# Requested weight groups, mixer products on VectorE, a new start, and Strassen's seven products in the down projection of a hybrid layer

## The chip, the cores and the metric

One Trainium2 chip, one NeuronCore. The metric is the device time of one execution in microseconds, as a median of repeated runs; the profile is of one further execution of the same program. TensorE (PE) multiplies 128x128 stationary tiles with moving tiles of up to 512 columns into PSUM; VectorE (DVE), ScalarE (ACT) and GpSimd (POOL) do elementwise work; SyncE (SP) issues the weight transfers.

## The reference

One layer over x of 256 x 2048 in float32. All sizes below are fixed: 11 chunks of 512 columns make the hidden width 5632.

```python
x = x + 0.5 * swiglu(rmsnorm(x, ffn1_norm), ffn1_w_gate, ffn1_w_up, ffn1_w_down)
h = rmsnorm(x, mix_norm)
x = x + mixer(h, rmsnorm(mem, mem_norm), ...)   # w_in, linear attention, spatial gating,
                                                # attention into 256 memory rows, w_branch, w_out
x = x + 0.5 * swiglu(rmsnorm(x, ffn2_norm), ffn2_w_gate, ffn2_w_up, ffn2_w_down)
return rmsnorm(x, final_norm)

def swiglu(h, w_gate, w_up, w_down):            # (2048, 5632), (2048, 5632), (5632, 2048)
    return (jax.nn.silu(h @ w_gate) * (h @ w_up)) @ w_down
```

## The kernel before

**Products in three parts.** A float32 operand is split into a high part of the type float32r (ACT's cast, `wh`, L119) and a low part (DVE's subtraction, `wl`, L120). A product of two tiles is then three PE matmuls: high x high, high x low, low x high (`products`, L123 to L125; in the Strassen blocks `three`, L364 for all). The weights come from memory in groups of four 128-row tiles by 512 columns (`load`, 1 MB, `raw`, a ring of three), requested on SP, and are split in halves of two tiles (`wh` and `wl`, rings of three). The tokens are two blocks of 128, so each half of a group is used in 12 matmuls.

**A feed-forward block (FFN)** walks over the 11 hidden chunks in parts of 4, 4 and 3 (`ffn`, L454). For each chunk it makes the gate and up products over 16 k tiles, the gated activation, four transposes for each token block (L166) and a split of the result into `hT` (`tsplit`, L174 and L175). After a part's last chunk it multiplies `hT` with the part's rows of `w_down`, for four groups of 512 output columns, and adds half of that into the tokens `x_s` (L486). Chunk 0 uses the plain `gemm`. Chunks 1 to 10 use `gated_strassen` (L348): the first four k tiles of the gate and of the up weights are taken as a 2 x 2 block matrix against the tokens' 2 x 2 blocks, with seven products (`p1` to `p7`, `seventh`) of sums of blocks instead of eight; the sums of the weight blocks are made on DVE (L413, 1024 columns wide) and split like weights; the sums of the token blocks are made once per FFN (`strassen_forms`, L313). The other 12 k tiles run as plain products (`rest`). The two first weight groups of a chunk (`rg`, `ru`) lie in slots of the pool `big` (17 slots of 8 KB per partition, `m` in the trace) and are requested when the chunk's code begins (L353).

**The mixer** (w_in, three branches, w_branch, w_out) runs small work of its branches in generators, one step at each half group (`tick`). The linear attention has seven levels; each makes two differences on DVE (L810, L811), an exponential on ACT (L812), one product on DVE (L814) and one on POOL (L815), all feeding small PE products (L795) and a masked copy on DVE (L799).

**The start** loads `mem` in four pieces and the first groups of `w_kv`; `norm_piece` (L182) transposes a piece on PE and makes its scaled high and low parts tile by tile (L190 on ACT, L191 on DVE). ACT also squares `mem` for the row sums (`mem_stats`, L257).

**Order.** Each engine runs its instructions in a fixed order; the order is made at build time by a scheduler that moves instructions of the program text ahead where their inputs allow. A pool's tile waits for the last reader of the slot it takes; SP and POOL requests wait in their queue for that too.

Of the kernel before, what the change touches and what calls it, by code (L numbers as in the profile page):

```python
# [8 lines left out]
F32 = mybir.dt.float32  # L9
# [50 lines left out]
def layer(ctx: ExitStack, tc: tile.TileContext, a: dict, out: bass.AP):  # L60
# [56 lines left out]

    def split(raw, wh, wl):
        nc.scalar.copy(wh, raw)  # L119
        nc.vector.tensor_tensor(wl, raw, wh.bitcast(F32), op=ALU.subtract)  # L120
# [119 lines left out]
    transposed_gains(gm, slice(0, KT))  # L240
    first = []
    for n in range(NCH):
# [4 lines left out]
        for b in range(NB):  # L247
            norm_piece(part[:, b, :], MEM, memT, None, b, n)
# [63 lines left out]

    def strassen_forms(xT):  # L313
# [18 lines left out]
    def gated(xT, rs, wg, wu, col):  # L332
# [15 lines left out]
    def gated_strassen(xT, forms, rs, wg, wu, col, between):  # L348


        rg, ru, tt = (slot([P, 4, CW]) for _ in range(3))
        for r, w in ((rg, wg), (ru, wu)):
            nc.sync.dma_start(  # L353
                r, w[: 4 * P, col : col + CW].rearrange("(j p) n -> p j n", p=P)
            )
# [39 lines left out]
        def rest():  # L395

            for g0 in range(4, KT, 4):
                for w, accs in ((wg, (p2, p4)), (wu, (p3, p8))):
                    raw = load(w, g0 * P, col)
                    for h0 in (0, 2):  # L400
                        wh, wl = ring(raw[:, h0 : h0 + 2, :])
                        last = g0 + h0 == KT - 2
# [10 lines left out]
        add = lambda o, x, y: nc.vector.tensor_tensor(o, x, y, op=ALU.add)  # L413
        sub = lambda o, x, y: nc.vector.tensor_tensor(o, x, y, op=ALU.subtract)
# [10 lines left out]

        c11, c21 = tmp(), tmp()
        e = slot([P, 2, CW])
        nc.scalar.copy(c11, p1)
        sub(e[:, 0], p6, c11)
        sub(c21, e[:, 0], p7)  # L430
        add(e[:, 0], e[:, 0], p5)
        add(e[:, 1], c21, p5)
        between()
# [5 lines left out]
        seventh(p4, tile_of(2, 1), own(t3), False)  # L439
        for _ in others:  # L440
            pass
        add(c11, p2, c11)
# [10 lines left out]

    def ffn(xT, rs, wg, wu, wd, after, begin=lambda: None, final=False):  # L454
        done, forms = 0, None
        for part, n_ch in enumerate((4, 4, 3)):
# [8 lines left out]

            for c in range(n_ch):
                col = (done + c) * CW
                if done + c == 0:
                    tiles = gated(xT, rs, wg, wu, col)
                    forms = strassen_forms(xT)  # L470
                else:
                    tiles = gated_strassen(xT, forms, rs, wg, wu, col, turn)
# [3 lines left out]
            if part == 2:  # L476
                begin()
            for n in range(NCH):
# [5 lines left out]
                for b in range(NB):  # L484
                    xs = x_s[b][:, n * CW : (n + 1) * CW]
                    nc.vector.scalar_tensor_tensor(  # L486
                        out=xs, in0=pd[b], scalar=0.5, in1=xs, op0=ALU.mult, op1=ALU.add
                    )
# [133 lines left out]
    def spatial():  # L622
# [14 lines left out]
        for b in range(NB):  # L637
# [9 lines left out]
            nc.gpsimd.tensor_tensor(sv[:, b, :], sv[:, b, :], ln[:, 1, :], op=ALU.add)  # L647
# [135 lines left out]
    def linear_attention():  # L783
# [22 lines left out]
        for i, m in enumerate(LEVELS):  # L806
# [8 lines left out]
            nc.gpsimd.tensor_tensor(qk[:, 1], kT, e, op=ALU.mult)  # L815
# [59 lines left out]
    for b in range(NB):  # L875
        nc.gpsimd.tensor_tensor(r_s[:, b, :], r_s[:, b, :], on, op=ALU.mult)
# [103 lines left out]
```

## Time and profile before

| | |
|---|---|
| median of 3 runs | 2377.97 us (2376.36 to 2378.29) |
| profiled execution | 2376.76 us; its span from first to last instruction 2375.1 us |
| PE busy | 2348.6 us, 99% of the span |
| PE weight loads (beside the products) | 1940.5 us, 82% |
| DVE busy | 1527.3 us, 64% |
| ACT busy | 1136.7 us, 48% |
| POOL busy | 63.1 us, 3% |
| moved by DMA | 456 MB, mean 192 GB/s |

Busy shares are averages over the whole span. A PE instruction's own length (0.39 us for 512 columns) overlaps with its neighbours', so the pace is read from the distance between starts. `[x <-ENGINE ...]` behind a row is the idle time of the engine before it and what ended it.

### The profile page before, as it was taken

Reading aid. Unit: us, or ns where it says so; the run is one execution under the profiler, and the core shown is the slowest. Engines: PE = TensorE matmul, PEld = TensorE weight load, DVE = VectorE, ACT = ScalarE, POOL = GpSimd, SP = SyncE. Lnnn points to the kernel's source line nnn. Section 1 sums busy time; section 2 is a strip of 40 time slices with the busy share of each in tenths; the row PEclk is TensorE's granted clock in tenths of the full one; section 3 lists DMA queues with packets and bytes.
Section 4 is the critical chain, followed back from the end, with each engine's and each line's share of the span. In section 5 each row is a group of like instructions: output and inputs, shape, how many; then the busy total and the mean of one; then the engine's idle time right before and its main releaser. Section 6 shows DMA issues by size and latency. Waiting matters only on the chain.

```text
span 2375.1 us, 26552 instructions
## 1 busy us (share of the span) xinstructions
PE 2348.6 (99%) x10610; PEld 1940.5 (82%) x10610; DVE 1527.3 (64%) x1658; ACT 1136.7 (48%) x1347; POOL 63.1 (3%) x62
## 2 busy tenths in 40 slices
PE   8999999999999999999999999999999999999998
PEld 6878888888888888888788888888788888888886
DVE  5668746885676656556765555556677468756765
ACT  6544534554454544435444444445445345534444
POOL 0000000000000001001200000000000000000000
PEclk9999999999999999999999999999999999999999
DMA  7665556655655665444446555555555556556554
GB/s 260 215 224 179 195 185 204 213 181 182 208 191 164 201 216 206 171 158 169 166 160 217 192 194 194 187 186 187 203 181 207 179 195 213 195 177 213 195 178 142
DMA packets 224821, 456.00 MB, mean 192 GB/s; under 512 B 7348, under 2 KB 7416, under 8 KB 223544
## 3 DMA queue, kind: packets, MB, share of 16 engines
q1 hardware_dynamic: 222344, 442.56, 55.4%
q0 software_dynamic: 2352, 11.73, 1.4%
q8 instruction: 83, 1.36, 0.2%
q14 instruction: 42, 0.34, 0.0%
HBM read 447.97 MB, written 6.29 MB: 191 GB/s over the span
## 4 chain that ended last, share of the span: by engine, by line
PE 97%; DMA 1%; ACT 1%; issue 1%; DVE 1%; SPq 0%; ACTq 0%; POOLq 0%; POOL 0%; DVEq 0%
PE acc L364 31%; PE acc L124 19%; PE acc L125 19%; PE acc L123 19%; PE trp L364 2%; PE sml L364 2%; PE trp L166 2%; DMA m<-in_ffn_w_gate_dram 1%; PE sml L795 1%; DVE wl L120 0%; ACT wh L119 0%; PE sml L700 0%; PE sml L728 0%; DMA m<-in_mem_dram 0%; ACT tmp L180 0%
## 5 line engine op out<-in xcount | busy, mean ns | idle before, releaser
L120 DVE TENSOR_TENSOR wl<-raw,wh 128x1024 fp32r<-128x1024 f32 x748 | 928.7, 1243 | 734.5 <-ACT wh L119 732.6
L119 ACT CAST wh<-raw 128x1024 fp32r<-128x1024 f32 x748 | 786.7, 1053 | 1002.5 <-PE acc L125 677.3
L124 PE MATMUL acc<-wl,m 128*128 128x512 f32 x2032 | 796.4, 392 | 1.6 <-DVE wl L120 1.6
L125 PE MATMUL acc<-wh,m 128*128 128x512 f32 x2032 | 792.5, 391 | 0.1
L123 PE MATMUL acc<-wh,m 128*128 128x512 f32 x2032 | 729.4, 392 | 1.8 <-ACT wh L119 0.9
L364 PE MATMUL acc<-wh,m 128*128 128x512 f32 x2080 | 656.8, 391 | 5.8 <-ACT wh L119 5.8
L364 PEld LDWEIGHTS acc<-wh,m 128*128 128x128 f32 x2080 | 392.2, 189 | 87.3 <-ACT wh L119 6.2
L123 PEld LDWEIGHTS acc<-wh,m 128*128 128x128 f32 x2032 | 381.6, 188 | 82.2 <-ACT m L190 2.2
L124 PEld LDWEIGHTS acc<-wl,m 128*128 128x128 f32 x2032 | 382.1, 188 | 81.3 <-DVE wl L120 3.1
L125 PEld LDWEIGHTS acc<-wh,m 128*128 128x128 f32 x2032 | 381.9, 188 | 77.4 <-DVE m L191 0.5
L364 PE MATMUL acc<-wl,m 128*128 128x512 f32 x1040 | 408.0, 392 | 1.2 <-DVE wl L120 1.2
L364 PEld LDWEIGHTS acc<-wl,m 128*128 128x128 f32 x1040 | 196.4, 189 | 42.6 <-DVE wl L120 2.3
L119 ACT CAST m<-m 128x1024 fp32r<-128x1024 f32 x80 | 82.5, 1051 | 31.8 <-DVE m L413 29.7
L120 DVE TENSOR_TENSOR m<-m,m 128x1024 fp32r<-128x1024 f32 x80 | 96.3, 1220 | 0.1
L119 ACT CAST wh<-m 128x1024 fp32r<-128x1024 f32 x60 | 63.2, 1054 | 58.3 <-PE acc L364 51.2
L120 DVE TENSOR_TENSOR wl<-m,wh 128x1024 fp32r<-128x1024 f32 x60 | 73.3, 1222 | 14.8 <-ACT wh L119 14.7
L413 DVE TENSOR_TENSOR m<-m,m 128x1024 f32<-128x1024 f32 x60 | 73.1, 1219 | 0.1
L364 PE MATMUL trp<-m,m 128*128 128x512 f32 x240 | 66.3, 390 | 0.0
L190 ACT ACTIVATE m<-trp,gT 128x128 fp32r<-128x128 f32 x128 | 43.1, 363 | 22.6 <-PE trp L166 13.2
L364 PEld LDWEIGHTS trp<-m,m 128*128 128x128 f32 x240 | 45.2, 188 | 9.4
L174 ACT CAST m<-trp 128x512 fp32r<-128x512 f32 x64 | 36.3, 583 | 28.5 <-PE trp L166 28.5
L191 DVE SCALAR_TENSOR_TENSOR m<-trp,gT,m 128x128 fp32r<-128x128 f32 x128 | 41.4, 346 | 13.2 <-ACT m L190 12.2
(175 smaller groups left out, 1025.3 us busy)
## 6 DMA issues: line engine op xcount, KB each, us to landing
raw<-in_w_in_dram SPq DMA_DIRECT2D x96, 1024.0 KB, 5.0
raw<-in_ffn_w_down_dram SPq DMA_DIRECT2D x88, 1024.0 KB, 5.1
raw<-in_ffn_w_gate_dram SPq DMA_DIRECT2D x68, 1024.0 KB, 5.1
raw<-in_ffn_w_up_dram SPq DMA_DIRECT2D x68, 1024.0 KB, 5.1
raw<-in_w_branch_dram SPq DMA_DIRECT2D x24, 1024.0 KB, 5.1
m<-in_ffn_w_gate_dram SPq DMA_DIRECT2D x20, 1024.0 KB, 7.5
m<-in_ffn_w_up_dram SPq DMA_DIRECT2D x20, 1024.0 KB, 8.5
raw<-in_w_out_dram SPq DMA_DIRECT2D x16, 1024.0 KB, 5.1
```

The source lines that it names most:

```text
L119: nc.scalar.copy(wh, raw)
L120: nc.vector.tensor_tensor(wl, raw, wh.bitcast(F32), op=ALU.subtract)
L123: nc.tensor.matmul(acc, lhsT=lhs.h(kt, b), rhs=wh, start=first, stop=False)
L124: nc.tensor.matmul(acc, lhsT=lhs.h(kt, b), rhs=wl, start=False, stop=False)
L125: nc.tensor.matmul(acc, lhsT=lhs.l(kt, b), rhs=wh, start=False, stop=last)
L166: nc.tensor.transpose(out=ps[:, j * P : (j + 1) * P], in_=src[:, j * P : (j + 1) * P], identity=ident)
L174: nc.scalar.copy(hi, ps)
L190: nc.scalar.activation(dst.h(kt, b), pj, AF.Copy, scale=g)
L191: nc.vector.scalar_tensor_tensor(out=dst.l(kt, b), in0=pj, scalar=g, in1=dst.h(kt, b).bitcast(F32), op0=ALU.mult, op1=ALU.subtract,)
L364: nc.tensor.matmul(o, lhsT=lhs, rhs=rhs, start=o not in opened, stop=stop)
L413: add = lambda o, x, y: nc.vector.tensor_tensor(o, x, y, op=ALU.add)
L795: nc.tensor.matmul(pss[:, h * P : (h + 1) * P], lhsT=ks[:, h, b * P : (b + 1) * P], rhs=qs[:, h, b * P : (b + 1) * P], start=True, stop=True,)
```

## The change

It has five pieces.

- **Requests.** The two first weight groups of a Strassen chunk are requested by a function of their own (`first_four`) during the chunk before: for chunk 1 between the gate and the up products of chunk 0, where the token forms are now made too; for the others behind the seventh of the seven products.
- **Down products.** The block code becomes `block_product`, used by the gated chunks and by `down_strassen`. The latter takes two 512-column groups of `w_down` as the two columns of blocks, for parts 0 and 1 of each FFN (two pairs per part); part 2 stays as it was. The forms of `hT` are made once per part. Sums go straight into `x_s` with a factor of 0.5 or -0.5 (`into_x`).
- **Mixer.** Eleven 128x1024 elementwise operations move from POOL to DVE: two in the spatial gating, seven in the linear attention's levels, two on the gate `r_s`.
- **Start.** Twenty transposes of the identity into an unused PSUM tile stand before the first pieces; `mem_stats` is ordered behind the last cast of the first `w_kv` column group.
- **Norm pieces.** Except for the first piece of `mem`, a piece is scaled in one DVE product over four tiles, cast once on ACT and subtracted once on DVE.

```diff
+    def first_four(w1, w2, row, col1, col2):
+        raws = [slot([P, 4, CW]) for _ in range(2)]
+        for r, w, col in zip(raws, (w1, w2), (col1, col2)):
+            nc.sync.dma_start(
+                r, w[row : row + 4 * P, col : col + CW].rearrange("(j p) n -> p j n", p=P)
+            )
+        return raws
...
-    def norm_piece(src, which, dst, ss, b, n):
+    def norm_piece(src, which, dst, ss, b, n, bulk=True):
...
+        if bulk:
+            t = tmp().rearrange("p (j t) -> p j t", t=P)
+            g = gT[:, which * KT + 4 * n : which * KT + 4 * n + 4]
+            nc.vector.tensor_tensor(
+                t, ps.rearrange("p (j t) -> p j t", t=P),
+                g.unsqueeze(2).to_broadcast([P, 4, P]), op=ALU.mult,
+            )
+            hi, lo = dst.four(4 * n, b)
+            nc.scalar.copy(hi, t)
+            nc.vector.tensor_tensor(lo, t, hi.bitcast(F32), op=ALU.subtract)
+            return
...
+    idle = trp()
+    for _ in range(20):
+        nc.tensor.transpose(out=idle[:, :P], in_=ident, identity=ident)
...
         if c == 0:
-            mem_stats()
+            with tc.issue_after(casts[0].ins):
+                mem_stats()
...
-    def gated(xT, rs, wg, wu, col):
+    def gated(xT, rs, wg, wu, col, between):
...
             nc.scalar.activation(sil[b], pg[b], AF.Silu, scale=rs[:, b : b + 1])
+        between()
         pu = [acc() for _ in range(NB)]
...
-    def gated_strassen(xT, forms, rs, wg, wu, col, between):
-        rg, ru, tt = (slot([P, 4, CW]) for _ in range(3))
-        for r, w in ((rg, wg), (ru, wu)):
-            nc.sync.dma_start(
-                r, w[: 4 * P, col : col + CW].rearrange("(j p) n -> p j n", p=P)
-            )
+    def block_product(xT, n_tiles, forms, raws, w1, w2, row0, col1, col2, middle, prefetch):
+        rg, ru = raws
+        tt = slot([P, 4, CW])
...
+        middle(p1, p6, p7, p5)
         add(t3, t3, b21)
         seventh(p2, tile_of(2, 0), ring(b21), False)
         next(others)
         seventh(p3, form(3), ring(b22), False)
         next(others)
         seventh(p4, tile_of(2, 1), own(t3), False)
+        prefetch()
         for _ in others:
             pass
+        return (p2, p4), (p3, p8)
...
+    def down_strassen(hT, n_tiles, forms, raws, wd, row0, n, prefetch):
+        def middle(p1, p6, p7, p5):
+            v, u = tmp(), tmp()
+            nc.scalar.copy(v, p1)
+            into_x(0, n, v)
+            sub(v, p6, v)
+            sub(u, v, p7)
+            add(v, v, p5)
+            into_x(0, n + 1, v)
+            into_x(1, n, u, -0.5)
+            add(u, u, p5)
+            into_x(1, n + 1, u)
+        banks = block_product(
+            hT, n_tiles, forms, raws, wd, wd, row0, n * CW, (n + 1) * CW, middle, prefetch
+        )
+        for i in range(2):
+            for b in range(NB):
+                into_x(b, n + i, banks[i][b])
...
+            if part < 2:
+                hf = strassen_forms(hT)
+                more = first_four(wd, wd, done * CW, 0, CW)
...
+                down_strassen(hT, 4 * n_ch, hf, more, wd, done * CW, 0, fetch_down)
+                down_strassen(
+                    hT, 4 * n_ch, hf, more, wd, done * CW, 2,
+                    (lambda n: lambda: fetch(n))(done + n_ch),
+                )
+                done += n_ch
+                continue
...
-            nc.gpsimd.tensor_tensor(qk[:, 1], kT, e, op=ALU.mult)
+            nc.vector.tensor_tensor(qk[:, 1], kT, e, op=ALU.mult)
```

How the order of the instructions changes, at three places. First PE, at the end of chunk 0 of the first FFN: L123 to L125 (after: L125 to L127) are the last up products of chunk 0, `trp<-ident,tmp` the transposes of its gated result, L364 (after: L397) products of chunk 1. Before:

```order
L123 MATMUL acc<-wh,m_221 128x512
L124 MATMUL acc<-wl,m_221 128x512
L125 MATMUL acc<-wh,m_223 128x512
L166 MATMUL trp<-ident,tmp 128x128 x8
L364 MATMUL acc<-wh,m_220 128x512 x2
```

After:

```order
L127 MATMUL acc<-wh,m_220 128x512
L397 MATMUL acc<-wh,m_217 128x512 x2
L397 MATMUL acc<-wl,m_217 128x512
L397 MATMUL acc<-wh,m_219 128x512
...
L397 MATMUL acc<-wh,m_219 128x512
L168 MATMUL trp<-ident,tmp 128x128 x4
L397 MATMUL acc<-wh,m_217 128x512 x2
L168 MATMUL trp<-ident,tmp 128x128 x4
```

Twelve products of chunk 1 have moved ahead of the transposes. ACT at the same place (L338, after L365: the gate's Silu of chunk 0; `wh<-m` are casts of a first weight group of chunk 1; `m<-trp`, L174, after L176, are the casts of the transposed result). Before:

```order
L338 ACTIVATE tmp<-acc,rs_219 128x512 x2
L119 CAST wh<-raw 128x1024 x6
L174 CAST m_987<-trp 128x4x128 x2
L119 CAST wh<-m_1337 128x1024
L119 CAST wh<-raw 128x1024 x2
```

After:

```order
L365 ACTIVATE tmp<-acc,rs_216 128x512 x2
L121 CAST wh<-raw 128x1024 x6
L121 CAST wh<-m_1146 128x1024
L121 CAST wh<-raw 128x1024 x2
L121 CAST wh<-m_1146 128x1024
L176 CAST m_952<-trp 128x4x128 x2
```

Four casts for chunk 1 have moved ahead of those of the transposed result. Third, ACT at the program's start (L119, after L121: casts of `w_kv` weights; L190, after L203: high parts of the transposed `mem`; L180: squares of `mem`). Before:

```order
L180 ACTIVATE tmp,ss_m<-m_89 128x512 x2
L190 ACTIVATE m_91<-trp,gT 128x128
L119 CAST wh<-raw 128x1024
L190 ACTIVATE m_91<-trp,gT 128x128 x2
L119 CAST wh<-raw 128x1024
L190 ACTIVATE m_91<-trp,gT 128x128
```

After:

```order
L121 CAST wh<-raw 128x1024 x2
L203 ACTIVATE m_91<-trp,gT 128x128 x4
L121 CAST wh<-raw 128x1024
L203 ACTIVATE m_91<-trp,gT 128x128 x2
```

The squares are gone from here (they follow the eighth cast), and two weight casts stand ahead of the first high part.

## Rows read from the trace of the kernel before

**Rows 1.** The page, busy time of each engine over the span.

```profile
PE 2348.6 (99%) x10610; PEld 1940.5 (82%) x10610; DVE 1527.3 (64%) x1658; ACT 1136.7 (48%) x1347; POOL 63.1 (3%) x62
```

**Rows 2.** Chain of waits: start, length in us, what, number of instructions.

```profile
738.80 25.64 PE acc L364 x113
```

**Rows 3.** Waits of PE over the span: us in total, times, longest.

```profile
PE acc L364 <- ACT wh L119: 5.8, 2, 3.0
...
PE acc L124 <- DVE wl L120: 1.6, 3, 0.9
PE acc L364 <- DVE wl L120: 1.2, 2, 0.7
...
PE acc L123 <- ACT m L190: 0.8, 1, 0.8
```

**Rows 4.** Timeline of PE, end of chunk 0 in the first FFN: start, length.

```profile
153.00 0.60 PE L166 MATMUL trp<-ident,tmp 128*128 128x128 f32 x4
...
157.44 0.73 PE L364 MATMUL acc<-wh,m 128*128 128x512 f32 x2 [2.77 <-ACT wh L119]
...
163.31 0.39 PE L364 MATMUL trp<-m,m 128*128 128x512 f32 x1
```

**Rows 5.** Windows: length, busy us (instructions) by engine, PE's granted clock, DMA.

```profile
153.20:163.30 10.10, 6.20 (x22) 4.38 (x21) 8.97 (x9) 5.34 (x7) 0.00 (x0) 0.83 0.41 152
1686.90:1698.80 11.90, 7.91 (x24) 5.54 (x23) 10.40 (x11) 6.37 (x8) 0.00 (x0) 0.71 0.47 161
```

**Rows 6.** Timeline of PE, end of chunk 0 in the second FFN.

```profile
1686.69 0.60 PE L166 MATMUL trp<-ident,tmp 128*128 128x128 f32 x4
...
1691.41 0.93 PE L364 MATMUL acc<-wh,m 128*128 128x512 f32 x2 [2.99 <-ACT wh L119]
...
1698.83 0.63 PE L364 MATMUL acc<-wh,m 128*128 128x512 f32 x2
```

**Rows 7.** Timeline of ACT, end of chunk 0 in the first FFN.

```profile
153.64 0.59 ACT L174 CAST m<-trp 128x512 fp32r<-128x512 f32 x1 [7.55 <-PE trp L166]
...
155.39 1.04 ACT L119 CAST wh<-m 128x1024 fp32r<-128x1024 f32 x1
```

**Rows 8.** Windows as rows 5: part 0's down products; a gated Strassen chunk.

```profile
540.00:630.00 90.00, 90.00 (x403) 74.61 (x401) 47.64 (x46) 36.77 (x37) 0.00 (x0) 1.00 0.55 182
640.00:682.00 42.00, 42.00 (x187) 34.80 (x186) 32.06 (x32) 21.23 (x22) 0.00 (x0) 1.00 0.55 187
```

**Rows 9.** Groups by line and shape: count, busy us, mean ns, idle before.

```profile
L120 DVE TENSOR_TENSOR wl<-m,wh 128x1024 fp32r<-128x1024 f32 x60 | 73.3, 1222 | 14.8 <-ACT wh L119 14.7
L413 DVE TENSOR_TENSOR m<-m,m 128x1024 f32<-128x1024 f32 x60 | 73.1, 1219 | 0.1
L486 DVE SCALAR_TENSOR_TENSOR m<-acc,m 128x512 f32<-128x512 f32 x48 | 31.0, 683 | 7.8 <-PE acc L125 7.8
L323 DVE TENSOR_TENSOR m<-m 128x256 f32<-128x256 f32 x2 | 0.8, 414 | 0.0
```

**Rows 10.** Timeline of all engines, a level of the linear attention.

```profile
1131.88 3.44 POOL L815 TENSOR_TENSOR m<-m,m 128x1024 f32<-128x1024 f32 x1 [3.52 <-ACT m L812]
...
1132.98 3.43 DVE L120 TENSOR_TENSOR wl<-raw,wh 128x1024 fp32r<-128x1024 f32 x1
...
1136.47 0.50 PE L124 MATMUL acc<-wl,m 128*128 128x512 f32 x1 [0.38 <-DVE wl L120]
```

**Rows 11.** Timeline of PE and ACT at the program's start.

```profile
6.08 1.97 PE L166 MATMUL trp<-ident,m 128*128 128x128 f32 x8 [3.25 <-DMA m<-in_mem_dram]
...
8.68 1.22 PE L123 MATMUL acc<-wh,m 128*128 128x512 f32 x2 [0.62 <-ACT wh L119]
...
9.12 1.04 ACT L119 CAST wh<-raw 128x1024 fp32r<-128x1024 f32 x1
...
10.96 0.63 PE L123 MATMUL acc<-wh,m 128*128 128x512 f32 x1
11.38 1.05 PE L124 MATMUL acc<-wl,m 128*128 128x512 f32 x2
```

More of the change, by code (lines that the diff above doesn't have):

```diff
@@ L116, in load @@
         return raw
+    casts = []
     def split(raw, wh, wl):
-        nc.scalar.copy(wh, raw)
+        casts[:] = [nc.scalar.copy(wh, raw)]
         nc.vector.tensor_tensor(wl, raw, wh.bitcast(F32), op=ALU.subtract)
@@ L247, in layer @@
         for b in range(NB):
-            norm_piece(part[:, b, :], MEM, memT, None, b, n)
+            norm_piece(part[:, b, :], MEM, memT, None, b, n, bulk=n > 0)
         if n < 3:
@@ L395, in rest @@
         def rest():
-            for g0 in range(4, KT, 4):
-                for w, accs in ((wg, (p2, p4)), (wu, (p3, p8))):
-                    raw = load(w, g0 * P, col)
+            for g0 in range(4, n_tiles, 4):
+                for w, col, accs in ((w1, col1, (p2, p4)), (w2, col2, (p3, p8))):
+                    raw = load(w, row0 + g0 * P, col)
                     for h0 in (0, 2):
                         wh, wl = ring(raw[:, h0 : h0 + 2, :])
-                        last = g0 + h0 == KT - 2
+                        last = g0 + h0 == n_tiles - 2
                         for b in range(NB):
@@ L424, in gated_strassen @@
         next(others)
[L426 to L433, printed above, removed]
+        middle(p1, p6, p7, p5)
         add(t3, t3, b21)
@@ L439, in gated_strassen @@
         seventh(p4, tile_of(2, 1), own(t3), False)
+        prefetch()
         for _ in others:
             pass
+        return (p2, p4), (p3, p8)
+    def gated_strassen(xT, forms, raws, rs, wg, wu, col, between, prefetch):
+        c11, c21 = tmp(), tmp()
+        e = None
+        def middle(p1, p6, p7, p5):
+            nonlocal e
+            e = slot([P, 2, CW])
+            nc.scalar.copy(c11, p1)
+            sub(e[:, 0], p6, c11)
+            sub(c21, e[:, 0], p7)
+            add(e[:, 0], e[:, 0], p5)
+            add(e[:, 1], c21, p5)
+            between()
+        (p2, p4), (p3, p8) = block_product(
+            xT, KT, forms, raws, wg, wu, 0, col, col, middle, prefetch
+        )
         add(c11, p2, c11)
@@ L464, in turn, with fetch, make_ready @@
                 waiting.clear()
+            def fetch(c):
+                nonlocal raws
+                if c < 11:
+                    raws = first_four(wg, wu, 0, c * CW, c * CW)
+            def make_ready():
+                nonlocal forms
+                forms = strassen_forms(xT)
+                fetch(1)
             for c in range(n_ch):
@@ L468, in ffn @@
                 if done + c == 0:
-                    tiles = gated(xT, rs, wg, wu, col)
-                    forms = strassen_forms(xT)
-                else:
-                    tiles = gated_strassen(xT, forms, rs, wg, wu, col, turn)
+                    tiles = gated(xT, rs, wg, wu, col, make_ready)
+                else:
+                    more = (lambda n: lambda: fetch(n))(done + c + 1)
+                    tiles = gated_strassen(
+                        xT, forms, raws, rs, wg, wu, col, turn,
+                        more if c < n_ch - 1 else lambda: None,
+                    )
                 waiting.append((c, tiles))
@@ L484, in ffn @@
                 for b in range(NB):
[L485 to L488, printed above, removed]
+                    xs = into_x(b, n, pd[b])
                     if part == 2:
@@ L875, in layer @@
     for b in range(NB):
-        nc.gpsimd.tensor_tensor(r_s[:, b, :], r_s[:, b, :], on, op=ALU.mult)
+        nc.vector.tensor_tensor(r_s[:, b, :], r_s[:, b, :], on, op=ALU.mult)
     gla_gen = linear_attention()
```

21 lines of the change are left out of this document (17 added, 4 removed).

## The prediction

> **What bounds the kernel now.** I read the page first: TensorE (PE) is busy 2348.6 of 2375.1 us, VectorE (DVE) 64%, ScalarE (ACT) 48% [rows 1]. So the kernel is a stream of PE products, and time can come only from fewer products or from the places where the stream breaks. The chain of waits gives the price of one product: 113 of them, one behind the other, take 25.64 us, which is 0.227 us each at the full clock [rows 2]; one product's own 0.39 us is overlapped by its neighbours. The PE's waits say where the stream breaks [rows 3]: 7.0 us in four waits for an ACT cast or a DVE low part at Strassen products (L364), all four at the start of a chunk 1, 1.6 us for DVE's low parts elsewhere, 0.8 us at the start. The waits alone undercount the first of these, since the clock falls behind them, so I looked at the timeline there.
>
> At the end of chunk 0 of the first feed-forward block (FFN) the PE starts eight transposes at 153.00, is then idle 2.77 us up to 157.44, and reaches the first `trp` product at 163.31 [rows 4]. The windows view counts 22 PE instructions in that stretch, at a granted clock of 0.83, and 24 in the like stretch of the second FFN, at 0.71 [rows 5]; the level in between is 1.2 instead of 2.4 GHz for part of the stretch. In the first stretch eight transposes at about 0.1 us and 14 products at 0.227 would need 4.0 us, and 10.3 went by: 6.3 lost. In the second [rows 6], eight and 16 would need 4.4, and 12.1 went by: 7.7 lost. Together 14.0 us. The cause stands on ACT: it is idle 7.55 us until the transposes' result comes, because the casts of that result stand in its queue ahead of the next chunk's weight casts, and the cast of the first weight group begins only at 155.39 [rows 7]. Those transposes in turn wait for the gated product, which is the last thing chunk 0 makes; nothing of chunk 1 stands between.
>
> **The change, part by part.**
>
> *Down products.* A pair of output columns of a four-chunk part now takes 2 x 16 x 2 x 3 = 192 products. By the seven products it takes 7 x 2 x 3 = 42 for the first four k tiles and 12 x 2 x 2 x 3 = 144 for the rest: 186. Two pairs, two parts and two FFNs make eight blocks, so 48 products go, at 0.227 us: **-10.9 us**. This term is sure as long as PE stays the bound. What it costs elsewhere: a block has 19 splits where the pair had 16, four 1024-wide additions at 1.22 us, and twelve 512-wide operations at 0.68 where there were four [rows 9]; DVE so gets about 3 x 1.22 + 4 x 1.22 + 8 x 0.68 = 14 us per block, and 2.4 + 4 x 0.41 = 4.1 us of forms once per part. I price that at nothing, because the PE's 42.2 us per block cover it: the gated Strassen block has the same 19 splits, four additions and nearly as many narrow operations, and there DVE is busy 32.1 of 42 us, while the down stretch now uses 47.6 of 90 [rows 8]. In the gated stretches PE has no wait on the list but the four named [rows 3]. With the forms a part's last gated chunk goes to some 36 of 42. If that cover is gone (an addition ahead of a low part that PE needs), each such place costs a wait like the longest for DVE here, 0.9 us [rows 3], and a wait of 2.8 us costs 6.3 with the clock. Eight block starts are new; I put **+1 us** for all, with 0 and 10 as the ends.
>
> *Requests ahead.* The first weight groups of the next chunk are asked for during the chunk before, and in the new order the PE has twelve rest products of chunk 1 ahead of the transposes, ACT has four weight casts ahead of its two transposed casts. Both links of the chain above are broken. On SP the pair now stands ahead of all eight raw groups of the first FFN's chunk 0, in the second behind two of them (before: behind the third raw group of chunk 1); the raw groups behind it wait for it on SP, but three of them fit in their ring ahead of the PE, some 16 us of products. What is late next is DVE's gated product, which the twelve products (2.7 us) cover. Of the 14.0 us I take **-13.0**, since a low part can still be a little late; the ends are -14 (all of it) and -9 (one of the two keeps two thirds of its loss).
>
> *Mixer operations.* Eleven 128x1024 operations go from GpSimd (POOL) to DVE. Beside POOL's 3.44 us a DVE subtraction that takes 1.22 elsewhere takes 3.43, and a PE wait of 0.38 stands behind it [rows 10]. So DVE already pays about 2.2 us beside such an operation, and would pay 1.2 for doing it: a level of the linear attention is up to 1 us shorter on DVE, which has no idle time before these rows. Against it: two multiplications now stand in one piece ahead of the next low part. The DVE waits there are 1.6 us on the list; I take **-1.5**, with +4 (a wait of 0.9 at each of the five levels that stand close together) and -3 (the listed waits and as much again in ACT's casts behind them) as ends.
>
> *Start.* The squares of `mem` leave ACT's head, but two weight casts now stand ahead of the first transposed piece. ACT's second cast runs 9.12 to 10.16 now; the first piece then comes at about 10.2 and the first product at 10.5 instead of 8.68 [rows 11]: 1.9 us late. The twenty idle transposes begin where the PE now idles, so the clock may already be up: now products start 0.43 us apart at 10.96 (half pace), and ten of them at 0.227 instead save 1.8. The 0.8 us wait for ACT's piece [rows 3] goes with the squares. Sum **-1.0**, ends +2 and -3.
>
> The rows here show only that products still ran at half pace at 10.96, after eight transposes from 6.08 on and with waits between [rows 11]. The Trainium skill (TensorE: Matmul & The Clock Gate, Part 4: PE-mode transpose) says that transposes do not count as PE activity for the full clock. By that rule the idle transposes buy nothing, the start is 1 us worse than now instead of 1 better, and the whole would come out 2 us later; no row here decides it, since transposes never stood alone long enough.
>
> *Norm pieces in one operation* (a piece was four ACT and four DVE operations of 128 columns, and becomes one ACT cast and two DVE operations of 512): **nothing**; ACT has half its time free [rows 1], and PE waits for none of these pieces after the start. A loss of a few tenths would be inside the range.
>
> Sum: -10.9 - 13.0 - 1.5 - 1.0 + 1.0 = -25.4 us. The profiled execution took 2376.76 us (1.66 around the span), the median of the runs is 2377.97, so 2351.4 against the one and **2352.5** against the other.
>
> **Rivals.**
>
> *A, slower: every down block starts cold.* If the first products of a down block stand behind the transposes of the part's last chunk as chunk 1's did, each start costs 6.3 us: eight of them cost 50, and 2352.5 + 50 = 2402. It decides from about four such starts on (4 x 6.3 = 25). For it speaks that the forms need DVE and ACT at just that time, and `trp` banks must be free. Against it: the new order puts 30 rest products of the first such block ahead of its first seven-product sum, and in the gated blocks the same start is free of waits. 3%.
>
> *B, the long waits only move.* If ACT or DVE is held by the early groups and chunk 1 still starts late by half: 7 us come back, 2359.5. 8%.
>
> *C, DVE falls behind in the mixer.* DVE then has 11 x 1.2 = 13 us more in a stretch where it has no gap: +4 instead of -1.5, 2358. 14%.
>
> *D, the start gains nothing* (the clock stays at half pace to the first products, or ACT's two casts cost more): 2354.5. The rule of the Trainium skill named above would make it so. 20%, and not outside my own uncertainty of the forecast.
>
> *E, the prefetch does nothing and the blocks cost some*: only the products pay, 2376.8 - 10.9 + 10 = no change to the eye, about 2377. 2%.
>
> My forecast, all terms about as stated, 53%.
>
> **How the numbers follow.** The forecast with D spans 2347 to 2357 for about 73%; C and B reach to 2361. At the other end all lower bounds together are -10.9 - 14 - 3 - 3 = -31, 2347. The range 2346 to 2362 leaves out A, E and the worst of B and C. What a measurement of this kernel can tell from no change is about 0.2%, 4.8 us. A (3%) is slower, E (2%) the same; all else is faster by more than 0.6%: 0.95, 0.02, 0.03.
>
> **What would show it.** Right: some 48 fewer products; 12 products ahead of the transposes at the end of each FFN's chunk 0, no ACT wait of over 1 us on PE there, and the granted clock full through both stretches; DVE busy 75 to 85% in the down stretches with no PE wait; DVE's stretched subtractions gone from the mixer; the first product at about 10.5 us, at the full pace. Wrong: a wait of PE for DVE's low parts or ACT's casts at block starts, or a clock below 1.00 anywhere after the start; PE waits around the linear attention's levels larger than now.

## The result, and the profile of the changed kernel

| | before | changed |
|---|---|---|
| median of 3 runs | 2377.97 us | 2352.51 us (2351.67 to 2352.65) |
| profiled execution | 2376.76 us, span 2375.1 | 2352.65 us, span 2350.9 |
| DVE, ACT, POOL busy | 1527.3, 1136.7, 63.1 us | 1636.9, 1149.5, 28.4 us |

The ratio is 0.9894, with a 95% interval of 0.9871 to 0.9916: faster by 1.1%. The forecast was 2352.5 (2346 to 2362). The total agrees to the tenth, and that is luck: two terms were too large, one too small, and one piece that was priced at nothing is not nothing. The experiments below take them apart.

The page of the changed kernel, the line that answers to [rows 1]:

```profile
PE 2335.1 (99%) x10582; PEld 1931.6 (82%) x10582; DVE 1636.9 (70%) x1753; ACT 1149.5 (49%) x1294; POOL 28.4 (1%) x51
```

PE executes 28 instructions fewer: 48 products go and 20 transposes come. DVE has 110 us more and PE is still the bound. All waits of PE, as [rows 3] (total, times, longest):

```profile
PE trp L243 <- POOL ident masks.py:199: 2.5, 1, 2.5
PE acc L397 <- DVE wl L122: 2.0, 4, 0.8
PE acc L125 <- ACT m L203: 1.9, 1, 1.9
PE trp L397 <- ACT m L121: 0.4, 2, 0.2
```

The 5.8 us for ACT's weight casts are gone. Of the four waits for `wl`, two are at the ends of chunk 0 and two (0.5 us together) at 1804 and 2062 us. The windows of the end of chunk 0 (as [rows 5]), of two stretches of part 0's down blocks (as [rows 8]) and of five levels of the linear attention (length, then busy us of PE, PEld, DVE, ACT, POOL, granted clock, DMA share, GB/s):

```profile
153.00:163.00 10.00, 9.02 (x43) 6.82 (x42) 8.34 (x10) 5.86 (x7) 0.00 (x0) 1.00 0.31 107
...
536.00:578.00 42.00, 42.00 (x190) 34.75 (x189) 38.88 (x41) 23.32 (x26) 0.00 (x0) 1.00 0.59 201
578.00:620.00 42.00, 42.00 (x187) 34.78 (x186) 33.11 (x34) 18.77 (x20) 0.00 (x0) 1.00 0.53 177
...
1100.00:1150.00 50.00, 50.00 (x247) 42.10 (x246) 40.37 (x43) 28.63 (x29) 0.00 (x0) 1.00 0.51 169
```

At the end of chunk 0 PE starts 43 instructions at the full clock, where it started 22 at 0.83. In the down blocks DVE is busy 93% of one stretch and 79% of the next, and PE not idle for a moment. What is left at the end of chunk 0 stands on two timelines, of PE and then of DVE:

```profile
160.13 0.91 PE L397 MATMUL acc<-wh,m 128*128 128x512 f32 x3
161.25 0.49 PE L397 MATMUL trp<-m,m 128*128 128x512 f32 x1 [0.21 <-ACT m L121]
162.51 0.50 PE L397 MATMUL acc<-wl,m 128*128 128x512 f32 x1 [0.77 <-DVE wl L122]
```

```profile
158.38 1.22 DVE L377 TENSOR_TENSOR m<-m 128x1024 f32<-128x1024 f32 x1
159.51 1.22 DVE L377 TENSOR_TENSOR m<-m,m 128x1024 f32<-128x1024 f32 x1
160.64 0.69 DVE L177 TENSOR_TENSOR m<-trp,m 128x512 fp32r<-128x512 f32 x1
161.24 1.22 DVE L122 TENSOR_TENSOR wl<-raw,wh 128x1024 fp32r<-128x1024 f32 x1
```

The low part that PE wants at 161.7 starts only at 161.24, behind two sums of weight blocks and a low part of `hT`; its high part was cast by 160.26 (ACT, 159.20 plus 1.06).

**Where 24.2 us of span went.** I took, in both traces, the distance between the starts of neighbouring PE instructions, less the usual distance of their kind (0.227 us for a product), and summed that excess by stretches of 50 us. At the two ends of chunk 0 it falls from 6.2 to 1.6 and from 7.6 to 1.6: 10.6 together. Between 1100 and 1150 us it falls from 3.4 to 0.4: 3.0. The two new places at 1804 and 2062 us add 1.1. The start is worth 0.2. With 48 products (10.9) and 0.5 at the tail that makes 10.9 + 10.6 + 3.0 - 1.1 + 0.2 + 0.5 = 24.1.

### The profile page after: what moved, and what is told of

It is laid out like the page before. It is cut to its first block, busy times and chain, and to the rows that moved or that the text cites. A ratio compares the mean times of both kernels' runs of the same rounds, so it can differ in the third digit from the quotient of the medians.

```text
span 2350.9 us, 26485 instructions
## 1 busy us (share of the span) xinstructions
PE 2335.1 (99%) x10582; PEld 1931.6 (82%) x10582; DVE 1636.9 (70%) x1753; ACT 1149.5 (49%) x1294; POOL 28.4 (1%) x51
## 4 chain that ended last, share of the span: by engine, by line
PE 96%; DVE 2%; DMA 1%; issue 1%; ACT 0%; SPq 0%; ACTq 0%; POOLq 0%; POOL 0%; DVEq 0%
PE acc L397 41%; PE acc L125 15%; PE acc L126 15%; PE acc L127 15%; PE sml L397 3%; PE trp L397 3%; PE trp L168 2%; DMA m<-in_ffn_w_down_dram 1%; DVE wl L122 1%; PE sml L890 1%; DVE m L377 0%; PE sml L795 0%; PE sml L823 0%; DMA raw<-in_w_kv_mem_dram 0%; ACT wh L121 0%
## 5 line engine op out<-in xcount | busy, mean ns | idle before, releaser
L122 DVE TENSOR_TENSOR wl<-raw,wh 128x1024 fp32r<-128x1024 f32 x716 | 874.8, 1223 | 612.0 <-ACT wh L121 610.9
L121 ACT CAST wh<-raw 128x1024 fp32r<-128x1024 f32 x716 | 753.7, 1053 | 946.6 <-PE acc L127 504.4
L397 PE MATMUL acc<-wh,m 128*128 128x512 f32 x2912 | 913.0, 390 | 0.0
L397 PEld LDWEIGHTS acc<-wh,m 128*128 128x128 f32 x2912 | 546.4, 188 | 112.8 <-ACT wh L121 0.4
L126 PE MATMUL acc<-wl,m 128*128 128x512 f32 x1520 | 597.4, 393 | 0.0
L127 PE MATMUL acc<-wh,m 128*128 128x512 f32 x1520 | 594.0, 391 | 0.0
L397 PE MATMUL acc<-wl,m 128*128 128x512 f32 x1456 | 569.5, 391 | 2.0 <-DVE wl L122 2.0
L125 PE MATMUL acc<-wh,m 128*128 128x512 f32 x1520 | 549.8, 393 | 2.0 <-ACT m L203 1.9
L125 PEld LDWEIGHTS acc<-wh,m 128*128 128x128 f32 x1520 | 285.6, 188 | 61.1 <-ACT m L203 2.6
L127 PEld LDWEIGHTS acc<-wh,m 128*128 128x128 f32 x1520 | 285.8, 188 | 57.5 <-DVE m L204 0.2
L397 PEld LDWEIGHTS acc<-wl,m 128*128 128x128 f32 x1456 | 273.4, 188 | 59.3 <-DVE wl L122 3.4
L121 ACT CAST m<-m 128x1024 fp32r<-128x1024 f32 x112 | 115.7, 1051 | 43.5 <-DVE m L377 40.7
L122 DVE TENSOR_TENSOR m<-m,m 128x1024 fp32r<-128x1024 f32 x112 | 135.3, 1220 | 0.0
L121 ACT CAST wh<-m 128x1024 fp32r<-128x1024 f32 x84 | 88.5, 1054 | 90.6 <-PE acc L397 77.4
L397 PE MATMUL trp<-m,m 128*128 128x512 f32 x336 | 95.2, 390 | 0.4 <-ACT m L121 0.4
L397 PEld LDWEIGHTS trp<-m,m 128*128 128x128 f32 x336 | 63.1, 188 | 14.3 <-ACT m L121 1.3
L397 PE MATMUL sml<-m,m 128*128 128x512 f32 x168 | 47.8, 389 | 0.0
L397 PE MATMUL acc<-m,m 128*128 128x512 f32 x168 | 47.2, 393 | 0.0
L177 DVE TENSOR_TENSOR m<-trp,m 128x512 fp32r<-128x512 f32 x64 | 43.3, 685 | 2.2 <-ACT m L176 2.0
```

The costliest lines, as they stand in the source:

```text
L121: casts[:] = [nc.scalar.copy(wh, raw)]
L125: nc.tensor.matmul(acc, lhsT=lhs.h(kt, b), rhs=wh, start=first, stop=False)
L126: nc.tensor.matmul(acc, lhsT=lhs.h(kt, b), rhs=wl, start=False, stop=False)
L127: nc.tensor.matmul(acc, lhsT=lhs.l(kt, b), rhs=wh, start=False, stop=last)
L177: nc.vector.tensor_tensor(lo, ps, hi.bitcast(F32), op=ALU.subtract)
L397: nc.tensor.matmul(o, lhsT=lhs, rhs=rhs, start=o not in opened, stop=stop)
```

## The experiments

Each is the changed kernel with one edit or a few, timed in four or five runs (e8 in eleven). The kernel before, run beside them on the same chip, took 2376.8 to 2377.0 us. The runs of one version lie 0.4 to 3.1 us apart, and those of the changed kernel were taken apart from these (beside 2377.97 of the kernel before), so a difference of about 1 us against 2352.5 is not sure; where one matters, the traces are compared too.

| run | median us | against 2352.5 |
|---|---|---|
| e1 plain down products | 2362.84 (2362.35 to 2362.92) | +10.3 |
| e2 requests late | 2362.94 (2361.22 to 2363.64) | +10.4 |
| e3 mixer on POOL | 2354.55 (2354.43 to 2354.84) | +2.0 |
| e4 no idle transposes | 2349.64 (2349.26 to 2349.97) | -2.9 |
| e5 sixteen more | 2352.84 (2352.17 to 2353.80) | +0.3 |
| e6 e4, squares early | 2350.04 (2349.84 to 2350.68) | -2.5 |
| e7 pieces in fours | 2355.74 (2355.33 to 2356.63) | +3.2 |
| e8 e4, third part too, early sum | 2372.56 (2370.98 to 2374.10) | +20.1 |
| e9 e4, early sum | 2347.24 (2346.80 to 2347.43) | -5.3 |
| e10 e8, rest first | 2364.20 (2363.99 to 2365.38) | +11.7 |
| e11 eight idle transposes | 2350.20 (2349.75 to 2350.92) | -2.3 |
| e12 whole start of before | 2352.58 (2351.48 to 2353.36) | +0.1 |

### e1: the down products plain again

```diff
-            if part < 2:
+            if False:
...
+                if part < 2 and n == NCH - 1:
+                    fetch(done + n_ch)
```

> The changed kernel with the plain products of before in all three parts of the down projection; requests ahead, mixer and start as changed. Theory: the 48 products come back at 0.227 us, 10.9, and the 1.1 us of small new waits at block starts go, so 9.8 us more than the changed kernel, 2362.3. Rival: the blocks cost more than their small waits show (DVE work that delays others), then it is only 5 to 7 us slower, 2358 to 2360. Second rival: the blocks also help what stands around them, 11 or more, 2363.5 and up.

10.3 us slower, against 9.8 of the theory and 11 or more of the second rival. The blocks pay what their products cost, less a little. The two waits at 1804 and 2062 us are gone in its trace. That rival A's price is real, though it isn't paid here, is seen in e8.

### e2: the requests late again

```diff
-                        more if c < n_ch - 1 else lambda: None,
+                        lambda: None,
```

with `fetch(done + c)` at the head of each Strassen chunk, and likewise in the down blocks.

> The changed kernel with the two first weight groups of a chunk or block requested where its own code begins, as before; the token forms are still made between gate and up products of chunk 0. Theory: the early requests gave the 10.6 us at the two ends of chunk 0, so it is about 10.6 us slower, 2363, with the granted clock at its lower level again around 160 and 1690 us, and further waits of PE at down block starts. Rival: the new order (rest products ahead of the transposes, forms earlier) gave them, and the groups come early enough anyway: 0 to 3 us slower, 2352.5 to 2355.5, clock full.

10.4 us slower, as the theory has it. PE's waits over the span, and the end of chunk 0 in the windows view:

```profile
PE acc L397 <- ACT wh L121: 6.1, 2, 3.3
...
153.00:163.00 10.00, 6.60 (x25) 4.62 (x24) 8.87 (x9) 5.94 (x7) 0.00 (x0) 0.83 0.42 156
```

The picture of [rows 4, 5] is back, though the token forms are still made early. On SP the pair is issued at 147.57 and 148.12 behind a raw group, and lands 7.5 and 9.6 us later; PE waits from 154.4 to 157.2. So late requests alone bring the loss back, and the new place of the forms doesn't prevent it. What e2 doesn't hold fixed is the order: its eight transposes stand ahead of chunk 1's products again, and no run has early requests with the old order. The trace of before tells which link was last there (the chain at the first end, then ACT at the second):

```profile
147.80 7.51 DMA m<-in_ffn_w_gate_dram
```

```profile
1689.37 1.04 ACT L119 CAST wh<-m 128x1024 fp32r<-128x1024 f32 x1 [0.32 <-DMA m<-in_ffn_w_gate_dram]
```

At the first end the weight group lands at 155.31, when ACT has just finished the second cast of the transposed result (at 155.28); at the second ACT stands idle for 0.32 us until it lands. So the landing held the first weight cast there, and the casts of the transposed result ahead of it on ACT cost nothing more. The raw group that PE's next products need had landed at 152.60, but its cast stands on ACT behind that one (from 156.34), and PE starts at 157.44, when half of it is cast. In e2 the down blocks don't suffer, against the theory: only one place there has more than 0.4 us of excess.

### e3: the mixer's eleven operations on POOL

```diff
-            nc.vector.tensor_tensor(qk[:, 1], kT, e, op=ALU.mult)
+            nc.gpsimd.tensor_tensor(qk[:, 1], kT, e, op=ALU.mult)
```

and the same in the other two lines.

> The changed kernel with the eleven mixer operations back on GpSimd. Theory: they gave 3.0 us, seen as less excess of PE between 1100 and 1150 us, so 2355.5, with the 3.4 us low parts and a PE wait of some 0.4 us behind them back. Rival of the prediction's term: 1.5 us, 2354. Third: the other part of it came from the order around them, and nothing changes, 2352.5.

2.0 us slower by the medians; the theory said 3.0, the prediction's term 1.5. The stretch in the windows view, and the low parts within it (count, busy, mean ns, idle before):

```profile
1100.00:1150.00 50.00, 48.17 (x226) 39.30 (x225) 38.85 (x34) 25.82 (x26) 16.04 (x5) 1.00 0.50 169
```

```profile
L122 DVE TENSOR_TENSOR wl<-raw,wh 128x1024 fp32r<-128x1024 f32 x16 | 27.0, 1699 | 8.4 <-ACT wh L121 8.4
```

In the changed kernel the same row is:

```profile
L122 DVE TENSOR_TENSOR wl<-raw,wh 128x1024 fp32r<-128x1024 f32 x17 | 20.8, 1222 | 10.2 <-ACT wh L121 10.2
```

Beside POOL a low part takes 0.48 us longer on average, and PE starts 226 instructions instead of 247. In this stretch the excess is again 3.4 us, so 3.0 worse. The rest of the span gave 1.1 back: at the start the granted clock stays full from 8.48 us on in this execution, where the changed kernel's falls for 3.4 us, although the instructions of the start are the same in both. So 2 to 3 us are shown, and the third theory (the order gave it) falls.

In e3's timeline two of POOL's multiplications and the low parts beside them read:

```profile
1106.52 3.44 POOL L910 TENSOR_TENSOR m<-m,m 128x1024 f32<-128x1024 f32 x1 [27.18 <-ACT m L907]
1108.25 2.79 DVE L122 TENSOR_TENSOR wl<-raw,wh 128x1024 fp32r<-128x1024 f32 x1
...
1120.44 3.43 POOL L910 TENSOR_TENSOR m<-m,m 128x1024 f32<-128x1024 f32 x1 [3.53 <-ACT m L907]
1121.54 3.42 DVE L122 TENSOR_TENSOR wl<-raw,wh 128x1024 fp32r<-128x1024 f32 x1
```

Each low part ends 1.1 us after POOL's operation (at 1109.96 and 1123.87), whether it began 1.7 or 1.1 us behind that one's start. It so stood until POOL was done and then took about its usual 1.22 us. The Trainium skill (SBUF — State Buffer, Who interferes with whom) says that a DVE instruction with two inputs in SBUF contends with a GpSimd instruction that reads SBUF, and that this is an exclusive lock. These rows agree: the low part is blocked, not slowed. In the spatial gating it is POOL that waits: beside its first addition (from 924.32, 5.53 us) two low parts, at 925.24 and 926.38, take 1.22 each.

### e4, e5, e11: the twenty idle transposes

```diff
-    for _ in range(20):
+    for _ in range(8):            # e11; e4 has none
```

e5 keeps the twenty and adds sixteen behind the first piece's transposes:

```diff
             norm_piece(part[:, b, :], MEM, memT, None, b, n, bulk=n > 0)
+        if n == 0:
+            for _ in range(16):
+                nc.tensor.transpose(out=idle[:, :P], in_=ident, identity=ident)
```

> The changed kernel without the twenty transposes of the identity; the scheduler then puts two of the first piece's casts ahead of the second weight cast on ACT. Theory: the clock that they bring is lost again in the 1.9 us of idle PE before the first product, and from some 15 us on PE follows the weights: no change, 2352.5 within 0.7, with the granted clock at the lower level up to about 13 us. Rival (the transposes pay): 1.8 us slower, 2354.3. Second rival (they only delay the first product): 1 us faster, 2351.5.

> The changed kernel with sixteen further transposes of the identity behind the transposes of the first piece of mem, where PE is idle from 8.0 to 9.9 us. Theory: the clock that the first twenty raised is then kept, and the ten products that took 0.43 us each take 0.227: up to 1.7 us faster, 2350.8, with the granted clock full from about 7 us on. Rival: the transposes of the second piece, which now stand behind twelve of them, come later and what is won is lost: 2352.5 to 2354.

> The changed kernel with eight transposes of the identity instead of twenty. They end before the first piece of mem lands (about 5.6 us), and the scheduler's order on ACT is nearly that of the version without any. Theory: the twenty cost 2.9 us because they hold PE past the landing and move two weight casts ahead of the first piece; so eight cost nothing: 2349.6. Rival: idle transposes cost by themselves (by the clock that falls behind them, or by their bank): 2351 or more. Second rival: they raise the clock early and nothing loses it: 2348.

Without them the kernel is 2.9 us faster, with eight instead of twenty 2.3 faster, with sixteen more than twenty the same. My theory for e4 (no change) fell: they cost. The start on PE in the changed kernel, and then without the idle transposes:

```profile
2.75 4.41 PE L257 MATMUL trp<-ident 128*128 128x128 f32 x20
6.99 1.04 PE L168 MATMUL trp<-ident,m 128*128 128x128 f32 x8
9.93 0.50 PE L125 MATMUL acc<-wh,m 128*128 128x512 f32 x1 [1.90 <-ACT m L203]
10.27 0.58 PE L126 MATMUL acc<-wl,m 128*128 128x512 f32 x1
10.65 0.63 PE L125 MATMUL acc<-wh,m 128*128 128x512 f32 x1
11.08 0.63 PE L126 MATMUL acc<-wl,m 128*128 128x512 f32 x1
```

```profile
5.67 1.97 PE L168 MATMUL trp<-ident,m 128*128 128x128 f32 x8 [2.84 <-DMA m<-in_mem_dram]
8.20 1.32 PE L125 MATMUL acc<-wh,m 128*128 128x512 f32 x2 [0.56 <-ACT wh L121]
```

Without them the transposes of the first piece start at 5.67, as soon as it has landed. With them PE is held by idle transposes until 6.99, and in the scheduler's order two weight casts stand ahead of the piece's casts on ACT. The first product so comes 1.7 us later. What the transposes were to bring is there for a moment only (windows of the changed kernel; the number behind POOL's is the granted clock):

```profile
8.00:10.30 2.30, 0.40 (x3) 0.33 (x3) 1.88 (x2) 1.58 (x4) 0.00 (x0) 1.00 1.02 371
10.30:13.70 3.40, 3.40 (x10) 2.60 (x9) 2.65 (x6) 2.09 (x5) 0.00 (x0) 0.50 1.05 396
```

At 8 us the granted clock is full (2.4 GHz), and the eight transposes at 6.99 run at about 0.11 us apart, where the twenty took 0.21. Then PE is idle for 1.9 us, and the products behind run 0.43 apart at 1.2 GHz up to 13.7. In e5 the clock is full from 5.6 us on, PE is still idle 1.6 us before the first product, and the clock falls at 12.5 until 15.9; a bridge without a gap was not tried. The profiled executions of e4 and the changed kernel are 3.4 us apart: some 2.2 lie at the start (excess there, with the wait for the first piece: 9.8 in the changed kernel, 7.5 in e4) and 1.1 at 1804 and 2062 us, where e4, e6, e7, e9, e11 and e12 have no wait. These two waits begin with a late landing. In the changed kernel DVE reads, 10 us ahead of the first:

```profile
1794.66 1.23 DVE L377 TENSOR_TENSOR m<-m 128x1024 f32<-128x1024 f32 x1 [1.45 <-DMA m<-in_ffn_w_down_dram]
```

The second group of the down block's pair lands 10.8 us after its request there (10.9 at the other place), in e4 after 9.6 and 9.8, and DVE then works without a pause up to the low part that PE waits for. The order is not the cause: behind 1700 us PE, DVE and ACT have the same sequence of work in both, by the names of their tiles. In all versions with the twenty transposes this group lands after 10.5 to 11.0 us, in e4, e6, e9, e11 and e12 after 9.4 to 10.0. Why is not shown, and e7 has the transposes and the late landing (10.6 and 10.5) without a wait.

The Trainium skill (TensorE: Matmul & The Clock Gate, Part 4: PE-mode transpose) says that transposes don't count as PE activity for the full clock. The trace disagrees for these, in float32: the clock was full at 8 us after nothing but transposes. That they bring nothing came out as by the rule, but by another mechanism, and the whole isn't 2 us later, since other pieces won more than forecast.

### e6, e7, e12: squares and pieces

e6 is e4 with the squares unheld; e7 has the pieces of 128 columns everywhere; e12 has both edits without the idle transposes, the whole start of before.

```diff
-            with tc.issue_after(casts[0].ins):          # e6, e12
-                mem_stats()
+            mem_stats()
...
-    def norm_piece(src, which, dst, ss, b, n, bulk=True):   # e7, e12
+    def norm_piece(src, which, dst, ss, b, n, bulk=False):
```

> The changed kernel without the twenty transposes and with the squares of mem where they stood before; only the norm pieces in one operation are left of the new start. Theory: without the transposes the kernel took 2349.6, and it was the squares' new place that gave this 2.9 us, since PE waits of 1.2 us at 19 and 0.5 at 21 us are gone there; so 2352.5 here, with such waits back. Rival: the norm pieces in one operation gave it, and the squares' place is worth nothing: 2349.6.

> The changed kernel with every norm piece as four ACT and four DVE operations of 128 columns, as before. Theory: nothing, 2352.5 within 0.7, as the prediction has it. Rival: at the start the pieces stand between the weight casts on ACT, and the longer ones bring back waits of PE between 15 and 30 us: 1 to 3 us slower, 2353.5 to 2355.5.

> The changed kernel with the whole start of before: no transposes of the identity, the squares where they were, pieces in four operations of 128 columns. Theory: by the traces the 96th product comes at the same time before and after, so the new start as a whole is worth nothing: 2352.5 within 0.7. Rival: the single runs add up (transposes 2.9 us worse than none, the squares' place 0.4 better, pieces in one operation 3.2 better): 2353.3; both within a microsecond, so what tells more is whether waits of PE for weights' casts or for pieces come back between 15 and 35 us.

The squares' place is worth 0.4 us, inside the spread: the theory for e6 fell, its rival holds. The pieces in one operation, which the prediction and e7's theory priced at nothing, are worth 3.2 with the squares held back and 2.5 without (e12 less e6). In e7 PE waits (timeline of PE, then of ACT):

```profile
31.80 0.50 PE L125 MATMUL acc<-wh,m 128*128 128x512 f32 x1 [1.46 <-ACT m L203]
```

```profile
30.79 0.61 ACT L182 ACTIVATE tmp<-m 128x512 f32<-128x512 f32 x1
31.31 0.19 ACT L182 ACTIVATION_READ_ACCUMULATOR tmp<-m 128x1 f32 x1
31.40 0.35 ACT L203 ACTIVATE m<-trp,gT 128x128 fp32r<-128x128 f32 x1
```

A piece's casts, one of 128 columns at a time, stand between the squares. In e12, without the hold, the waits are at 8 (0.6) and 19 us (0.8). Together the new start is worth 0.1 us by the medians, nothing within 1 us: what the pieces win the idle transposes lose.

### e8, e9, e10: what is left, and the third part

The first sum of chunk 1 moves into `make_ready`; e8 and e10 also give the third part's down projection the seven products (both pairs in the first FFN, one in the second); e10 puts three half groups of the rest first in those blocks. Unlike the blocks of parts 0 and 1, whose next pair is asked for during the block before, each of these asks for its pair in its own code.

```diff
                 fetch(1)
+                tt = slot([P, 4, CW])
+                add(tt[:, 2:4], raws[1][:, 0:2], raws[1][:, 2:4])
+                raws.append(tt)
...
+            pairs = 1 if final else 2                       # e8, e10
+            hf = strassen_forms(hT)
+            for n in range(0, 2 * pairs, 2):
+                more = first_four(wd, wd, done * CW, n * CW, (n + 1) * CW)
+                down_strassen(hT, 4 * n_ch, hf, more, wd, done * CW, n, lambda: None)
...
+        if n_tiles == 12:                                   # e10
+            for _ in range(3):
+                next(others)
```

> The changed kernel without the twenty transposes, with the first sum of weight blocks of each chunk 1 made between the gate and up products of chunk 0, and with the seven products in the third part as well (both column pairs in the first feed-forward block, the first pair in the second). Theory: 2349.6, less 18 products at 0.227 us, 4.1, less what is left at the two ends of chunk 0, where a DVE sum of 1.2 us stands ahead of a low part that PE waits for, 2 to 3 us: 2342.5 to 2343.5. Rival: the sum is not what is late, and only the products pay: 2345.5. Second rival: the blocks of the third part meet the norm pieces behind them on DVE and cost as much as they save: 2347 to 2349.

> The changed kernel without the twenty transposes and with the first sum of each chunk 1 made between the gate and up products of chunk 0; the third part is left as it was. Theory: the profile of the version with the third part changed as well had no wait left at the two ends of chunk 0, where 1.6 us each were left; so 2349.6 - 3.2 = 2346.4. Rival: those 3.2 us only move to the chunk behind: 2349.6.

> As the version with the seven products in the third part as well, but in a block of the third part three half groups of the rest (36 products) now come first in the code, so that 24 of them stand ahead of the last chunk's transposes and ACT has weight casts to do meanwhile. Theory: those blocks lost some 27 us to cold starts, because nothing of the block stood ahead of the transposes; with the cover nearly all of that goes and the 18 products pay: 2346.4 - 4.1 = 2342.3, up to 2345 if a small wait is left at each of the three. Rival: the blocks of the third part are late for another reason (their weight requests, made only at the block's start): 2360 or more.

e9 is the fastest: 2347.24 us, a ratio of 0.9876 to the kernel before (0.9862 to 0.9889). The excess at both ends of chunk 0 is zero, and the end of chunk 0 reads (window; after it all of PE's waits over the span):

```profile
148.00:163.00 15.00, 15.00 (x72) 12.44 (x71) 11.75 (x13) 8.78 (x10) 0.00 (x0) 1.00 0.41 136
```

```profile
PE trp L168 <- DMA m<-in_mem_dram: 2.9, 1, 2.9
PE trp L243 <- POOL ident masks.py:199: 2.5, 1, 2.5
PE acc L125 <- ACT wh L121: 0.6, 1, 0.6
```

It is 2.4 faster than e4 by the medians, where 3.2 were expected. Between the profiled executions it is 2.1: the 3.2 at the two ends are gone, and the start is 1.1 slower (clock full from 14.8 us instead of 12.5). So the mechanism is as stated; whether the start takes the rest in the medians too is not shown.

e8 met none of its three expectations. It is 25.3 slower than e9, though it saves 18 products (4.1): three starts lost some 29 us (excess of 10.5, 7.6 and 11.3). The windows of the three:

```profile
749.00:762.00 13.00, 5.06 (x19) 3.13 (x18) 11.64 (x16) 5.61 (x7) 0.00 (x0) 0.76 0.40 147
793.00:804.00 11.00, 6.19 (x22) 4.16 (x21) 10.76 (x14) 6.86 (x10) 0.54 (x1) 0.69 0.63 247
2283.00:2297.00 14.00, 6.05 (x22) 3.89 (x21) 12.50 (x17) 6.11 (x7) 0.00 (x0) 0.70 0.39 146
```

This is rival A of the prediction, with its lower clock, in a place that the change doesn't touch. In e10 36 products come first in a block and 8 us of the 29 go; PE then waits 4.8 us at the same point. ACT and SP there:

```profile
761.43 1.04 ACT L352 CAST m<-m 128x1024 fp32r<-128x1024 f32 x1 [3.46 <-DVE m L350]
762.38 1.04 ACT L121 CAST wh<-m 128x1024 fp32r<-128x1024 f32 x1
```

```profile
733.86 16.73 SPq L112 DMA_DIRECT2D raw<-in_ffn_w_down_dram  x4
750.65 1.05 SPq L332 DMA_DIRECT2D m<-in_ffn_w_down_dram  x2
```

My theory (only cover is missing) fell; 2364.2 lies where the rival put it, but the rival's reason, the late request, is what comes last at one of the three starts alone. At the first start the pair is issued at 750.65 behind four raw groups that wait for their ring. Its first group lands at 758.75, and ACT casts it only at 762.38, behind the cast of the token forms, which waits for DVE's last form (L350, up to 761.41). The third start has the same chain (forms' cast at 2291.57). At the second start the forms are there, and ACT waits for the pair, which lands 11.0 us after its request at 790.81:

```profile
801.95 1.04 ACT L121 CAST wh<-m 128x1024 fp32r<-128x1024 f32 x1 [3.97 <-DMA m<-in_ffn_w_down_dram]
```

In part 0 of the changed kernel the pair is issued at 519.28, ahead of its raw groups. No run mends one of the two, the forms' path or the request, alone.

## Why the prediction was right, point by point

- **Down products, -10.9 and +1 for new starts:** right. e1 measures 10.3 net, the trace 10.9 less 1.1. That DVE's extra work is covered was right even at 93% of DVE. The 1.1 hang on a late landing at two of the eight blocks, and six versions with the same blocks don't have them. By the prediction's own words (a wait of PE for DVE's low parts at block starts) they, and the 0.8 us at each end of chunk 0, are signs of being wrong; they are small ones.
- **Requests ahead, -13.0:** that earlier requests remove the loss was right (e2), the size too large: 10.6 by the trace, 10.4 by e2. The reading "the cause stands on ACT" was half right: a raw group's cast stood in ACT's queue, but behind the cast of the first weight group, which waited for its landing (155.31 and 1689.29) and not for the casts of the transposed result. So the late request was the link to mend. The step of the size that failed is "what is late next is DVE's gated product". Late next are DVE's weight sums, which stand ahead of a low part, 1.6 us at each end; moving one sum removes it (e9).
- **Mixer, -1.5:** the right sign, too small: 2.0 by e3's medians, 3.0 in the stretch. The prediction counted a level's 1 us on DVE and the listed waits (1.6 us); the excess of PE there was 3.4, so PE's starts behind stretched low parts lose more than the listed waits show.
- **Start, -1.0, and norm pieces, nothing:** together -0.1 (e12), so rival D's outcome for this term, by two errors that cancel. (Its own terms, 1.9, -1.8 and -0.8, add up to -0.7, not -1.0.) The idle transposes cost 2.3 to 2.9 instead of winning 1.8: the step "the clock may already be up" was true at 8 us, but it was gone again at 10.3 after the idle time before the first product, and that they delay the first piece was not counted. The first product came at 9.93, about as forecast, but at half pace. The pieces in one operation win 2.5 to 3.2; "PE waits for none of these pieces after the start" was the wrong row to price them by, since at the start it does.
- **Rivals:** A did not occur in the change's own blocks, but does in the third part's (e8). B and C did not come: no long wait is left in the chunks, and DVE keeps up in the mixer.

Of the forecast's -25.4 us the profiled executions show -24.1: the requests gave 2.4 less and the start 0.8 less, the mixer 1.5 more, and 0.5 at the tail was not forecast. The medians differ by 25.5, since before's profiled run lies 1.2 below its median. So the match to the tenth is luck.

## What to carry to other kernels

Where a stall sits at the first product of a stage, look at which engine's queue holds the work that would feed it, and request and prepare that work a stage earlier; then read the same place again, because the next late thing can be one short operation ahead of the needed one (here a 1.2 us sum on DVE). Filler work on an idle engine can delay the real work when that arrives early. Saved products are worth their full time only where each block's start is covered: the same algorithm won 10.3 us in two parts and lost 25 in the third.

## What the runs showed of the hardware that I had not expected

Transposes alone raised TensorE's granted clock (full before 8 us, after twenty of them 0.21 us apart; the eight behind ran 0.11 us apart), and it fell again after 1.9 us without work, for 3.4 us in which ten products ran at 0.43 us. With the same instructions at the start, the clock of another execution (e3, full from 8.48 us, 1.25 us without work) did not fall, which made 1.1 us: a part of the spread between runs may come from there. And each DVE subtraction with two inputs in SBUF that began during a POOL multiplication of the linear attention (e3) ended 1.1 us after that one's end, whenever it had begun: it was blocked and not slowed.
